# Sums of squares in column groups, wider rows of x, and four dots of the first shift on TensorE

## Chip, core and metric

The kernel runs on one core of a Trainium2 chip. The metric is the time of one execution on the device in microseconds (us); times are medians of three runs. Profiles show one execution: TensorE (PE) with its weight loads (PEld), VectorE (DVE), ScalarE (ACT), GpSimd (POOL), and the DMA queue of SyncE (SP).

## What is computed

Two layers over 1024 tokens of 1024 channels, in fp32, the first with a convolution as token mixer, the second with a pooling mixer:

```python
s = silu(c)
for i in range(2):
    sh, sc, gt = split(s @ w_mod[i] + b_mod[i], 3)
    h = rms(x, norm_g[i]) * (1 + sc) + sh
    if i == 0:                                   # _conv_mixer
        a, b, g = split(h @ w_in, 3)
        y = depthwise_conv31(a * sigmoid(b)) + db
        o = (silu(layernorm(y)) * silu(g)) @ w_out
    else:                                        # _pool_mixer
        v, g = split(h @ w_in, 2)
        p = window_means(v, (2, 4, 8, 16)) - v
        o = (grouped(p @ w_grp) * scale * silu(g)) @ w_out
    x = x + gt * o
```

`rms` and `layernorm` divide each token by the root of a mean of squares over its 1024 channels.

## The kernel before

Channels lie on the partitions, tokens along a row. x is a set of eight blocks of 128 channels, each in two halves `h` of 512 tokens. A product in fp32 is three matmuls (`mm3`, L200 to L203): each factor is split into a high and a low part of the type fp32r, a cast (`hi_part`, line L164 or L165, ScalarE) and a subtraction (`lo_part`, L169 or L170, VectorE or GpSimd). So `h10h` and `h10l` are the parts of the modulated x of half 1, blocks 0 and 1; `w00h` and `w00l` those of a weight.

Program order: load x of half 0 (eight DMAs of 256 KB), its norm, and block by block the modulation `mod_block` (two dots of `s_row`, the row of silu(c), with a block of `w_mod`, one for the shift and one for the scale, each one VectorE instruction, L287), `x <- x * a * rb` (L366), and `h`; seven accumulations `pf` on TensorE take up each block as it comes. Then half 1 is normed in the same way (`vax`, `vpx`, `rbx`), and the `pg` products use both halves. The 31 taps of the convolution run as products `pr` on ScalarE with adds `z` on GpSimd (L471, L472) and as `cv` chains on VectorE (L484); TensorE goes through the other products (`ps`, `psg`) meanwhile. `layernorm` follows for each half: means by `mr` and `mu`, squares `sqz`, their sums `vpz`, `rbz`. Then `gate_norm`, `out_half` (products `pso`, which give the x of the second layer, whose squares are `sqy`, sums `vpy`, factor `rby`), `h2_half`, and the second layer with `psv`, `psq`, `psy`, `psf`.

Five norms need, for each token, a sum over 1024 channels, that is over partitions as well. There are two forms. In `squares` (x0, x1, y1) VectorE adds up the squares of the eight blocks (L266) and four matmuls with a moving operand of a single column add over the partitions; y1 keeps its last block apart and has eight. In `square_sums` (z0, z1, y0) each block of squares has its own four such matmuls (L277), the block being the stationary operand. Both leave the sums as 128 x 4. `rstd_rows` turns these into the factor: ScalarE adds eps (`ve`, L240), GpSimd takes the power -0.5 (`vr`, L242), ScalarE spreads it on four diagonals (`dg`, L247), one matmul makes a row block of it (`rb`, L248). Names carry the norm: `vex`, `vry`, `dgz`.

Four tile pools matter: PSUM tag "ax" is one single bank (sums, `rb`, `gv`), "mm" has five and "cv" two; the SBUF ring for squares, "sq", has two buffers, as has that of the products, "pr".

The order on each engine is fixed when the program is built: a scheduler takes instructions by priority, by its own estimate of when they are ready (`priority(-LATER)` puts the norms first; `behind` and `ordered` add constraints). On the chip each engine takes its list in that order and waits at an instruction whose operands aren't there. An edit in one place therefore reorders others.

## Time and profile before

| what | value |
|---|---|
| median of three runs | 758.52 us (757.62 to 759.13) |
| the profiled execution's own time | 758.71 us |
| its span, first to last instruction | 756.9 us |
| TensorE busy | 724.2 us (96%) |
| VectorE busy | 532.1 us (70%) |
| ScalarE busy | 386.4 us (51%) |
| GpSimd busy | 435.4 us (58%) |
| chain that ended last, by engine | PE 70%, DVE 14%, POOL 8%, ACT 3% |

A busy share is a mean over stages that differ. Where a stretch of the trace shows one engine busy all the time, that engine sets the pace there; elsewhere one looks for what it waits for.

### The profile page before, as it was taken

How to read it: one execution, taken by the hardware profiler on the slowest of the kernel's cores; microseconds unless marked ns; L12 is line 12 of the kernel's file. 1: busy time of each engine (PE TensorE's matmuls, PEld its weight loads, DVE VectorE, ACT ScalarE, POOL GpSimd, SP SyncE). 2: the span in 40 equal slices, each digit the busy share in tenths (PEclk: the TensorE clock that was granted, in tenths of full speed). 3: DMA queues.
4: the chain of work that ended last, by engine and by line, in shares of the span. 5: the costliest groups of instructions: out<-in, count | busy, mean ns of one | idle time of the engine just before them, and what ended most of it. 6: DMA issues, size and time to landing. Idle time of an engine off the chain costs nothing.

```text
span 756.9 us, 9894 instructions
## 1 busy us (share of the span) xinstructions
PE 724.2 (96%) x3572; PEld 574.1 (76%) x3572; DVE 532.1 (70%) x724; ACT 386.4 (51%) x576; POOL 435.4 (58%) x377
## 2 busy tenths in 40 slices
PE   3899999999999999999989989999999999999998
PEld 1677786676768788778766768788888788888997
DVE  5997997889898941589969989671737364477321
ACT  5355556656613346876886676652414433334110
POOL 2000889999913438899998999763117413344232
PEclk9999999999999999999999989999999999999999
DMA  8882006466323441643650132445625610334132
GB/s 324 315 318 82 0 1 249 167 223 233 132 82 98 152 153 63 202 140 113 207 171 24 57 126 83 154 168 160 203 92 203 200 56 28 98 112 140 56 126 72
DMA packets 36481, 105.68 MB, mean 140 GB/s; under 512 B 4048, under 2 KB 6224, under 8 KB 36432
## 3 DMA queue, kind: packets, MB, share of 16 engines
q1 hardware_dynamic: 36432, 105.05, 40.8%
q8 instruction: 28, 0.46, 0.2%
q14 instruction: 21, 0.17, 0.1%
HBM read 92.45 MB, written 12.58 MB: 139 GB/s over the span
## 4 chain that ended last, share of the span: by engine, by line
PE 70%; DVE 14%; POOL 8%; ACT 3%; issue 2%; DMA 2%; SPq 0%; DVEq 0%; POOLq 0%; ACTq 0%
POOL z L472 8%; PE ps L201 4%; PE ps L203 4%; PE ps L202 4%; PE psf L202 4%; PE psf L203 4%; PE psf L201 4%; PE psv L203 3%; PE psv L202 3%; PE psv L201 3%; PE psq L202 3%; PE psq L201 3%; PE psq L203 3%; PE psg L203 3%; PE psg L201 3%; PE psg L202 3%
## 5 line engine op out<-in xcount | busy, mean ns | idle before, releaser
L472 POOL TENSOR_TENSOR z<-z,pr 128x512 f32<-128x512 f32 (+8 forms) x210 | 297.1, 1415 | 49.4 <-ACT pr L471 21.2
L471 ACT ACTIVATE pr<-y,VT 128x512 f32<-128x512 f32 (+8 forms) x210 | 150.2, 719 | 96.8 <-POOL z L472 90.2
L484 DVE SCALAR_TENSOR_TENSOR cv<-y,VT,cv 128x512 f32<-128x512 f32 (+12 forms) x261 | 175.4, 741 | 0.4
L770 DVE SCALAR_TENSOR_TENSOR xf<-psf,gt,xf 128x260 f32<-128x260 f32 (+1 forms) x24 | 13.2, 570 | 36.9 <-PE psf L203 31.4
L753 DVE SCALAR_TENSOR_TENSOR q<-psy,VT,q 128x260 f32<-128x260 f32 (+1 forms) x24 | 13.6, 571 | 31.9 <-PE psy L203 31.7
L242 POOL TENSOR_TENSOR vrx<-vex,mhalf 128x4 f32<-128x4 f32 x2 | 2.1, 1026 | 57.2 <-ACT vex L240 57.2
L567 DVE TENSOR_TENSOR z<-z,rbz 128x512 f32<-128x512 f32 x16 | 10.7, 680 | 28.9 <-PE rbz L248 28.9
L671 DVE TENSOR_TENSOR s<-v 128x535 f32<-128x535 f32 x8 | 12.3, 1536 | 19.5 <-ACT v L719 19.5
L675 DVE TENSOR_TENSOR s<-s 128x517 f32<-128x517 f32 (+5 forms) x24 | 20.9, 870 | 0.6
L559 ACT ACTIVATE gn<-z,VT 128x512 f32<-128x512 f32 x16 | 12.4, 777 | 14.6 <-DVE z L567 14.4
L287 DVE SCALAR_TENSOR_TENSOR wmb<-wmb,s_row 128x1024 f32<-128x1024 f32 x16 | 19.4, 1220 | 0.0
L583 DVE SCALAR_TENSOR_TENSOR xr<-pso,gt,xr 128x512 f32<-128x512 f32 x16 | 11.5, 741 | 10.7 <-PE pso L203 10.7
L299 PE MATMUL gv<-wk,srep 128*32 128x256 f32 x256 | 18.6, 388 | 0.0
L164 ACT CAST y<-q 128x504 fp32r<-128x504 f32 (+1 forms) x16 | 9.9, 618 | 16.8 <-DVE q L753 16.8
L169 DVE TENSOR_TENSOR y<-q,y 128x504 fp32r<-128x504 f32 (+1 forms) x16 | 13.9, 869 | 3.6 <-ACT y L164 3.6
L277 PEld LDWEIGHTS vpz<-ones,sqz 128*128 128x128 f32 x128 | 15.5, 191 | 0.7
L275 ACT ACTIVATE sqz<-z 128x512 f32<-128x512 f32 x16 | 9.8, 629 | 12.0 <-PE vpz L277 11.5
L202 PE MATMUL psy<-pd,grs 128*128 128x260 f32 (+1 forms) x48 | 15.3, 320 | 0.0
L203 PE MATMUL psy<-pd,grs 128*128 128x260 f32 (+1 forms) x48 | 15.3, 319 | 0.0
L201 PE MATMUL psy<-pd,grs 128*128 128x260 f32 (+1 forms) x48 | 15.1, 318 | 0.0
L277 PE MATMUL vpz<-ones,sqz 128*128 128x1 f32 x128 | 14.7, 245 | 0.0
L169 DVE TENSOR_TENSOR grs<-gr,grs 128x512 fp32r<-128x512 f32 x8 | 9.1, 1132 | 8.0 <-ACT grs L164 8.0
(2503 smaller groups left out, 2352.6 us busy)
## 6 DMA issues: line engine op xcount, KB each, us to landing
wk<-in_wk SPq DMA_DIRECT2D x32, 512.0 KB, 5.1
wmb<-in_wm SPq DMA_DIRECT2D x16, 512.0 KB, 6.4
wo<-in_cv_wo SPq DMA_DIRECT2D x16, 512.0 KB, 3.5
wp<-in_pl_wo SPq DMA_DIRECT2D x16, 512.0 KB, 3.5
wg<-in_cv_w SPq DMA_DIRECT2D x12, 512.0 KB, 3.7
wv<-in_pl_w SPq DMA_DIRECT2D x12, 512.0 KB, 3.4
wq<-in_pl_w SPq DMA_DIRECT2D x12, 512.0 KB, 3.5
x<-in_xT SPq DMA_DIRECT2D x16, 256.0 KB, 6.2
```

The lines of the kernel that those rows point to most:

```text
L169: return eng.tensor_tensor(out=lo, in0=src, in1=hi.bitcast(F32), op=ALU.subtract)
L201: nc.tensor.matmul(ps, w[0], r[0], start=first, stop=False)
L202: nc.tensor.matmul(ps, w[0], r[1], start=False, stop=False)
L203: nc.tensor.matmul(ps, w[1], r[0], start=False, stop=last)
L277: nc.tensor.matmul(vp[:, j : j + 1], sq[:, bl(j)], ones[:, 0:1], start=i + j == 0, stop=i == KT - 1, skip_group_check=True,)
L287: nc.vector.scalar_tensor_tensor(out=w, in0=w, scalar=1.0, in1=s_row, op0=ALU.mult, op1=ALU.mult, accum_out=out)
L299: nc.tensor.matmul(ps[32 * q : 32 * q + 32, :256], srep[:, kt, :], w[:, 256 * q : 256 * q + 256], start=kt == 0, stop=kt == KT - 1,)
L471: nc.scalar.activation(pr[:, o], y[:, i], AF.Copy, scale=dw(k))
L472: nc.gpsimd.tensor_tensor(out=z[:, o], in0=z[:, o], in1=pr[:, o], op=ALU.add)
L484: nc.vector.scalar_tensor_tensor(out=a[:, o], in0=y[:, i], scalar=dw(k), in1=a[:, o], op0=ALU.mult, op1=ALU.add)
L675: nc.vector.tensor_tensor(out=s[:, :m], in0=s[:, :m], in1=s[:, step : step + m], op=ALU.add)
L753: mixed[0] = nc.vector.scalar_tensor_tensor(out=sg[m][:, piece], in0=ps, scalar=vcol(ct, V_PS), in1=sg[m][:, piece], op0=ALU.mult, op1=ALU ...
```

## The change

1. All five norms take their sums by `token_sums`: for each block of squares four matmuls with a stationary operand of 32 columns of `onesd` (all 1/1024), each on another quarter of the 512 tokens, written to another 32 partitions of PSUM: four column groups. The result is 128 x 128, a token in each column of a group. `squares` with its adds on VectorE goes.
2. `rstd_rows` therefore gets two more steps: a copy `vrow` of the 128 x 128 with eps (ScalarE) and a matmul with `sel` that picks one row of each group and gives 128 x 4; `ve` becomes a copy.
3. x is laid out by the host so that two blocks lie side by side in one row: four DMAs of 512 KB with rows of 4 KB in place of eight of 256 KB with rows of 2 KB, in `load_x` and in `out_half`.
4. For the blocks 1 to 4 (`SH_PE`) the dot for the shift leaves VectorE. `dot_pe` has eight matmuls with `srep` (32 equal columns of silu(c)) in four column groups, over the block of `w_mod` in another layout, a copy `shrow` on ScalarE, and a matmul with `selm` that adds the groups; VectorE adds the bias from PSUM.

```diff
@@ -27,6 +27,7 @@
 CORD = [ct for p in PAIRS for ct in p]
 FILL = (4, 6, 5, 7)
 MIX_AT = 4
+SH_PE = (1, 2, 3, 4)
 EARLY_W = (1, 1, 2, 2)
 EARLY_AT = (0, 2, 1, 1)
 EARLY_ENG = ((0, 0, 0, 0), (1, 1, 1, 1))
...
-    RINGS = {"w": 4, "raw": 4, "sg": 2, "sq": 2, "pr": 2, "vs": 1}
+    RINGS = {"w": 4, "raw": 4, "sg": 2, "sq": 2, "pr": 2}
     WIDTH = {"E": 2 * NB, "Z": 2 * (NB + 2 * PAD), "sg": NB + 2 * PAD, "pr": NB}
     LATER = 1 << 20
     tc.cur_priority = 4 * LATER
@@ -101,13 +102,6 @@
 
     def bl(j):
         return slice(j * P, (j + 1) * P)
-
-    def packed(tags, name):
-        res = []
-        for j, tag in enumerate(tags):
-            u = unit(tag, f"{name}{j}")
-            res += [u[:, hs(0)], u[:, hs(1)]]
-        return res
 
     def pair(region, i, name):
         return unit(f"{region}{i}", name + "h", F32R), unit(f"{region}{i + 1}", name + "l", F32R)
@@ -222,24 +216,22 @@
 
     power_done, spread_done = [None], [None]
 
-    def rstd_rows(total, name):
-
-
-        sums, vp = total
-        if vp is None:
-            vp = axps(f"vp{name}")
-            with priority(-LATER):
-                for i, summed in enumerate(sums):
-                    for j in range(4):
-                        nc.tensor.matmul(
-                            vp[:, j : j + 1], summed[:, bl(j)], ones[:, 0:1], start=i + j == 0,
-                            stop=i == len(sums) - 1, skip_group_check=True,
-                        )
-        ve = S.tile([P, 4], F32, tag="ve", name=f"ve{name}", bufs=2)
+    def token_sums(ps, src, first, last):
+
+
+        for j in range(4):
+            nc.tensor.matmul(ps[32 * j : 32 * j + 32, :P], onesd[:, :32], src[:, bl(j)], start=first, stop=last)
+
+    def rstd_rows(vp, name):
+
+        row = S.tile([P, P], F32, tag="vrow", name=f"vrow{name}", bufs=1)
+        rs = S.tile([P, 4], F32, tag="vr", name=f"vr{name}", bufs=2)
         with priority(-LATER):
-            nc.scalar.activation(ve, vp[:, 0:4], AF.Identity, scale=1.0 / D, bias=eps)
-        rs = S.tile([P, 4], F32, tag="vr", name=f"vr{name}", bufs=2)
-        power_done[0] = nc.gpsimd.tensor_tensor(out=rs, in0=ve, in1=mhalf[:, 0:4], op=ALU.pow)
+            nc.scalar.activation(row, vp[:, :P], AF.Identity, bias=eps)
+            nc.tensor.matmul(vp[:, P : P + 4], row, sel, start=True, stop=True)
+            ve = S.tile([P, 4], F32, tag="ve", name=f"ve{name}", bufs=2)
+            nc.scalar.copy(ve, vp[:, P : P + 4])
+            power_done[0] = nc.gpsimd.tensor_tensor(out=rs, in0=ve, in1=mhalf[:, 0:4], op=ALU.pow)
         rb = axps(f"rb{name}")
         dg = half("sq", f"dg{name}")
         with priority(-LATER):
@@ -249,38 +241,16 @@
         spread_done[0] = spread
         return rb, done
 
-    def squares(xs, name, apart=False):
-
-        total = half("vs", f"va{name}")
-        sums = [total]
-
-        def add(i):
-            if i == 0:
-                nc.scalar.activation(total, xs[i], AF.Square)
-                return None
-            sq = half("sq", f"sq{name}{i}")
-            nc.scalar.activation(sq, xs[i], AF.Square)
-            if apart and i == KT - 1:
-                sums.append(sq)
-                return None
-            return nc.vector.tensor_tensor(out=total, in0=total, in1=sq, op=ALU.add)
-
-        return (sums, None), add
-
     def square_sums(xs, name, vp):
 
 
         def add(i):
             sq = half("sq", f"sq{name}{i}")
             done = nc.scalar.activation(sq, xs[i], AF.Square)
-            for j in range(4):
-                nc.tensor.matmul(
-                    vp[:, j : j + 1], sq[:, bl(j)], ones[:, 0:1], start=i + j == 0, stop=i == KT - 1,
-                    skip_group_check=True,
-                )
+            token_sums(vp, sq, i == 0, i == KT - 1)
             return done
 
-        return (None, vp), add
+        return vp, add
 
     def dot(w, out):
 
@@ -320,12 +290,14 @@
     xs = [None, None]
 
     def load_x(h):
-        xs[h] = packed([f"{'FZ'[h]}{j}" for j in range(4)], f"x{h}")
-        for kt in range(KT):
-            load_next(xs[h][kt], xT[bl(kt), hs(h)])
+        xs[h] = []
+        for j in range(4):
+            u = unit(f"{'FZ'[h]}{j}", f"x{h}{j}")
+            load_next(u, xT[h, j])
+            xs[h] += [u[:, hs(0)], u[:, hs(1)]]
 
     def norm_x(h):
-        total, add = squares(xs[h], f"x{h}")
+        total, add = square_sums(xs[h], f"x{h}", axps(f"vpx{h}"))
         for kt in range(KT):
             last = add(kt)
         return last, rstd_rows(total, f"x{h}")[0]
@@ -341,11 +313,26 @@
         nc.tensor.matmul(ps, ones, dg, start=True, stop=True)
         nc.scalar.copy(s_row[:, hs(h)], ps)
 
+    def dot_pe(kt, w):
+
+        ps = axps(f"sh{kt}")
+        row = S.tile([P, P], F32, tag="vrow", name=f"shrow{kt}", bufs=1)
+        with priority(-LATER):
+            for k in range(KT):
+                g = slice(32 * (k % 4), 32 * (k % 4) + 32)
+                nc.tensor.matmul(ps[g, :P], srep[:, k, :], w[:, bl(k)], start=k < 4, stop=k >= 4)
+            nc.scalar.copy(row, ps[:, :P])
+            nc.tensor.matmul(ps[:, P : P + 1], row, selm[:, 0:1], start=True, stop=True)
+        return ps[:, P : P + 1]
+
     def mod_block(kt):
         dots = []
         for part in range(2):
             w = unit("w" if part else "raw", f"wmb{kt}{part}")
             load_next(w, wm[part, kt])
+            if part == 0 and kt in SH_PE:
+                dots.append(dot_pe(kt, w))
+                continue
             dots.append(S.tile([P, 1], F32, tag=f"dot{part}", name=f"dot{kt}{part}", bufs=2))
             dot(w, dots[part])
         nc.vector.tensor_tensor(out=sh0[:, kt : kt + 1], in0=dots[0], in1=vcol(kt, V_BM), op=ALU.add)
@@ -574,10 +561,12 @@
 
     def out_half(h, y1, ws, done, beside=None):
         group = len(ws)
-        x1 = packed([f"Z{j}" for j in range(4)], f"xr{h}")
-        for m in range(KT):
-            nc.sync.dma_start(out=x1[m], in_=xT[bl(m), hs(h)])
-        total, add = squares(x1, f"y{h}", True) if h else square_sums(x1, f"y{h}", axps("vpy0"))
+        x1 = []
+        for j in range(4):
+            u = unit(f"Z{j}", f"xr{h}{j}")
+            nc.sync.dma_start(out=u, in_=xT[h, j])
+            x1 += [u[:, hs(0)], u[:, hs(1)]]
+        total, add = square_sums(x1, f"y{h}", axps(f"vpy{h}"))
 
         def finish(m, ps):
             nc.vector.scalar_tensor_tensor(
@@ -857,11 +846,14 @@
     )
     wk = np.stack([g["w_mod"][i][:, j * D : (j + 1) * D] for i, j in ((0, 2), (1, 0), (1, 1), (1, 2))])
     wk = wk.reshape(4, KT, P, D)
+    wm = g["w_mod"][0].T.reshape(3, KT, P, D)[:2].copy()
+    for kt in SH_PE:
+        wm[0, kt] = wm[0, kt].reshape(P, KT, P).transpose(2, 1, 0).reshape(P, D)
     wf = g["cv_w_in"][0].reshape(KT, P, 3, D)[:, :, :2, : FIRST * P]
     arrays = {
-        "xT": g["x"][0].T,
+        "xT": g["x"][0].T.reshape(4, 2, P, 2, HW).transpose(3, 0, 2, 1, 4).reshape(2, 4, P, 2 * HW),
         "vecs": vecs,
-        "wm": g["w_mod"][0].T.reshape(3, KT, P, D)[:2],
+        "wm": wm,
         "wk": wk,
         "cv_first": wf.reshape(KT, P, 2 * FIRST * P),
         "cv_w": tiles(g["cv_w_in"][0]),
```

The lists of the engines change with it. TensorE at the end of the first `pf` stage, before (`rbx` carries the factor of half 1 to all partitions, `pg` are products of half 0 first and of `h10` after them):

```order
L202 MATMUL pf_200<-h06l,w07h 128x512
L203 MATMUL pf_200<-h06h,w07l 128x512
L248 MATMUL rbx_531<-dgx_532,ones 128x512
L201 MATMUL pg_628<-h00h,w00h 128x512
L202 MATMUL pg_628<-h00l,w00h 128x512
L203 MATMUL pg_628<-h00h,w00l 128x512
L201 MATMUL pg_628<-h00h,w01h 128x512
```

and after:

```order
L195 MATMUL pg_708<-h06h,w07h 128x512
L196 MATMUL pg_708<-h06l,w07h 128x512
L197 MATMUL pg_708<-h06h,w07l 128x512
L240 MATMUL rbx_611<-dgx_612,ones 128x512
L195 MATMUL pg_737<-h10h,w00h 128x512
L195 MATMUL pg_762<-h10h,w00h 128x512
L195 MATMUL pg_790<-h10h,w00h 128x512
L195 MATMUL pg_815<-h10h,w00h 128x512
L195 MATMUL pg_843<-h10h,w00h 128x512
```

Before, 24 matmuls of one `pg` on the blocks of half 0 follow `rbx` before the first with `h10h`; now these 24 stand ahead of `rbx`. Its `sel` stands 19 matmuls ahead of it.

VectorE at the same place, before (`x <- x,a,rbx` is the modulation of half 1, `cv` the convolution, `h10l` the low part for TensorE):

```order
L382 TENSOR_TENSOR y_588<-pf_195,sig_589 128x512
L480 TENSOR_SCALAR cv_1043<-y_588,VT 128x512
L480 TENSOR_SCALAR cv_1044<-y_588,VT 128x511
L370 SCALAR_TENSOR_TENSOR x_447<-x_447,a_128,rbx_531 128x512 x2
L370 SCALAR_TENSOR_TENSOR x_448<-x_448,a_128,rbx_531 128x512 x2
L370 SCALAR_TENSOR_TENSOR x_449<-x_449,a_128,rbx_531 128x512 x2
L370 SCALAR_TENSOR_TENSOR x_450<-x_450,a_128,rbx_531 128x512 x2
L484 SCALAR_TENSOR_TENSOR cv_1043<-y_588,VT,cv_1043 128x497
L482 MEMSET cv_1044 128x1
L170 SCALAR_TENSOR_TENSOR h10l<-x_447,sh_129,h10h 128x512 x2
```

and after:

```order
L471 SCALAR_TENSOR_TENSOR cv_1124<-y_668,VT,cv_1124 128x504
L369 TENSOR_TENSOR y_733<-pg_708,sig_734 128x512
L471 SCALAR_TENSOR_TENSOR cv_1123<-y_668,VT,cv_1123 128x505
L357 SCALAR_TENSOR_TENSOR x_507<-x_507,a_128,rbx_611 128x512 x2
L357 SCALAR_TENSOR_TENSOR x_509<-x_509,a_128,rbx_611 128x512 x2
L357 SCALAR_TENSOR_TENSOR x_511<-x_511,a_128,rbx_611 128x512 x2
L357 SCALAR_TENSOR_TENSOR x_513<-x_513,a_128,rbx_611 128x512 x2
L471 SCALAR_TENSOR_TENSOR cv_1124<-y_668,VT,cv_1124 128x506
L471 SCALAR_TENSOR_TENSOR cv_1123<-y_668,VT,cv_1123 128x507
L164 SCALAR_TENSOR_TENSOR h10l<-x_507,sh_129,h10h 128x512 x2
```

The eight x's stand behind nine `cv` and behind a `y` that reads a finished `pg`, and two `cv` instead of one stand between them and `h10l`.

TensorE near the second norm of half 1, before (`psf` are products of the second layer, `rby` the factor of y1):

```order
L202 MATMUL psf_5077<-y_4007,wp70h 128x504
L203 MATMUL psf_5077<-y_4007,wp70l 128x504
L201 MATMUL psf_5077<-y_4018,wp70h 128x504
L202 MATMUL psf_5077<-y_4018,wp70h 128x504
L203 MATMUL psf_5077<-y_4018,wp70l 128x504
L248 MATMUL rby_4997<-dgy_4998,ones 128x512
L201 MATMUL psf_5077<-y_4196,wp70h 128x504
```

and after:

```order
L197 MATMUL psf_5179<-y_4089,wp70l 128x504
L195 MATMUL psf_5179<-y_4100,wp70h 128x504
L196 MATMUL psf_5179<-y_4100,wp70h 128x504
L197 MATMUL psf_5179<-y_4100,wp70l 128x504
L231 MATMUL vpy_4779<-sel,vrowy_5092 128x4
L240 MATMUL rby_5099<-dgy_5100,ones 128x512
L195 MATMUL psf_5179<-y_4278,wp70h 128x504
L196 MATMUL psf_5179<-y_4278,wp70h 128x504
```

Before, 14 matmuls lie between the last sums `vpy` and `rby`; now 11 lie between the last sums and `sel`, and none between `sel` and `rby`. In the other norms the squares' sums move too: those of x1 from one block behind 147 matmuls of `pf` to eight blocks behind 84 to 148; those of z0 by 5, 10 and 15 matmuls back. On ScalarE `dgy` of y0 comes behind the cast `wv20h`, which it stood ahead of, and on GpSimd `vry` of y0 stands behind five more of the convolution's z's.

## Rows read from the trace of the kernel before

**Rows 1.** The page: busy time of each engine, share, instructions.

```profile
PE 724.2 (96%) x3572; PEld 574.1 (76%) x3572; DVE 532.1 (70%) x724; ACT 386.4 (51%) x576; POOL 435.4 (58%) x377
```

**Rows 2.** Stretches: length, busy time (records) of PE, PEld, DVE, ACT, POOL, clock, DMA, GB/s.

```profile
22.80:62.00 39.20, 38.10 (x156) 30.04 (x157) 37.87 (x66) 17.42 (x24) 0.00 (x0) 1.00 0.84 310
85.00:225.00 140.00, 140.00 (x779) 101.54 (x780) 125.63 (x189) 77.34 (x114) 116.50 (x86) 1.00 0.41 147
390.00:470.00 80.00, 73.87 (x302) 56.07 (x302) 74.76 (x85) 56.60 (x88) 74.32 (x76) 0.96 0.24 79
448.00:452.00 4.00, 3.56 (x8) 2.82 (x9) 2.25 (x3) 2.73 (x5) 3.87 (x4) 0.50 0.42 134
610.00:757.00 147.00, 143.31 (x850) 126.76 (x848) 68.87 (x90) 40.47 (x56) 45.39 (x44) 1.00 0.27 87
```

**Rows 3.** Waits of TensorE: who, for whom, us in total, times, longest.

```profile
PE pf L201 <- ACT h00h L165: 2.2, 1, 2.2
PE psv L203 <- DVE wv40l L169: 3.7, 1, 3.7
```

**Rows 4.** Time line of TensorE: start, us, engine, line, operation, records [idle before].

```profile
122.28 0.39 PE L202 MATMUL ps<-h04l,wb4h 128*128 128x512 f32 x1
122.50 0.40 PE L203 MATMUL ps<-h04h,wb4l 128*128 128x512 f32 x1
122.83 0.64 PE L299 MATMUL gv<-wk,srep 128*32 128x256 f32 x8
123.40 0.51 PE L201 MATMUL ps<-h04h,wb4h 128*128 128x512 f32 x1
123.74 0.39 PE L202 MATMUL ps<-h04l,wb4h 128*128 128x512 f32 x1
...
141.74 0.50 PE L308 MATMUL gv<-sel,row 128*128 128x4 f32 x4
142.10 0.49 PE L203 MATMUL ps<-h16h,wb4l 128*128 128x512 f32 x1
...
148.05 1.93 PE L299 MATMUL gv<-wk,srep 128*32 128x256 f32 x32
149.91 0.50 PE L201 MATMUL ps<-h00h,wb5h 128*128 128x512 f32 x1
...
349.19 0.95 PE L277 MATMUL vpy<-ones,sqy 128*128 128x1 f32 x8
350.00 0.47 PE L201 MATMUL pso<-y100h,wo06h 128*128 128x512 f32 x1
```

**Rows 5.** Time line of VectorE and ScalarE, end of the squares of x0.

```profile
10.59 3.08 DVE L266 TENSOR_TENSOR vax<-vax,sqx 128x512 f32<-128x512 f32 x4 [0.20 <-ACT sqx L262]
11.45 1.30 ACT L262 ACTIVATE sqx<-x 128x512 f32<-128x512 f32 x2
```

**Rows 6.** Time line of three engines around `rbx` of x1.

```profile
66.66 1.02 PE L248 MATMUL rbx<-dgx,ones 128*128 128x512 f32 x2
68.63 5.35 DVE L370 SCALAR_TENSOR_TENSOR x<-x,a,rbx 128x512 f32<-128x512 f32 x8
69.40 1.38 ACT L165 ACTIVATE h10h<-x,sh 128x512 fp32r<-128x512 f32 x2 [1.15 <-DVE x L370]
74.54 0.75 DVE L170 SCALAR_TENSOR_TENSOR h10l<-x,sh,h10h 128x512 fp32r<-128x512 f32 x1
75.35 0.50 PE L202 MATMUL pg<-h10l,w00h 128*128 128x512 f32 x1 [1.16 <-DVE h10l L170]
```

**Rows 7.** Time line of GpSimd and VectorE ahead of the second layer.

```profile
384.08 8.21 POOL L472 TENSOR_TENSOR z<-z,pr 128x512 f32<-128x512 f32 x5 [0.36 <-ACT pr L471]
389.04 2.10 DVE L169 TENSOR_TENSOR wv20l<-wv,wv20h 128x1024 fp32r<-128x1024 f32 x1 [2.93 <-ACT wv20h L164]
```

**Rows 8.** Time line of ScalarE, the factor of y1.

```profile
599.68 0.26 ACT L240 ACTIVATE vey<-vpy,eps 128x4 f32<-128x4 f32 x1 [5.23 <-PE vpy L234]
601.07 1.28 ACT L247 ACTIVATE dgy<-ident,vry 128x128 f32<-128x128 f32 x4 [1.12 <-POOL vry L242]
```

## The prediction, made before the changed kernel ran

> **What bounds the kernel now.** I read the page's busy line first: TensorE works in 724.2 of 756.9 us, 96% of the span [rows 1]. The page names a list of lines, none of them dominant, so the question is where the other engines set TensorE's pace. The table of stretches tells it: from 85 to 225 us TensorE is busy 140.0 of 140 us, from 610 to 757 us 143.31 of 147, but from 390 to 470 us only 73.87 of 80, while VectorE is at 74.76 and GpSimd at 74.32 [rows 2]. So in most of the program a microsecond of TensorE is a microsecond of time, and around 390 to 450 us it is not: there TensorE waits, the longest time 3.7 us for VectorE's `wv40l` [rows 3]. Behind that wait the granted clock reads 0.50 from 448 to 452 us [rows 2], 1.2 of 2.4 GHz: an idle stretch of that length costs twice.
>
> **What a block of sums costs on TensorE.** Fixed first, since every part uses it. Plain 512-column matmuls start 0.22 to 0.23 us apart. One group of four narrow matmuls (128 x 32 weights, 256 columns, 8 records) takes 0.57 us from its start to the next start; the start before it comes 0.10 late and the second one behind it 0.11 late: 0.78 in all [rows 4]. Four groups in one run take 1.86 us start to start, so a further group costs (1.86 - 0.57)/3 = 0.43 and each visit a fixed 0.35. The new groups have half the columns, 128. I take 0.43/2 = 0.22 for one, 0.56 for a visit with one group and 0.78 with two. Bounds: 0.22 (no fixed part) and 0.78 (columns don't matter). An old block of four one-column matmuls takes 0.81 and about 0.1 of border: 0.9; a pair 1.8. Two `sel` matmuls of four columns take 0.36 [rows 4]; I take that for each `sel` and `selm`.
>
> The Trainium skill ("TensorEngine Tiling (Array Packing)", Theoretical Speedup) gives up to a factor of four for a stationary of at most 32 columns, and its Key Properties say that a change of tiling mode drains the engine. The rows show 0.9 against 0.56, a factor of 1.6; with the factor of four, 0.22 a block, the sum would be that of rival 1.
>
> **A. The start, to the end of the seven `pf` accumulations.** Before, the first norm's last square ends at 11.45 + 1.30 = 12.75 us and the last add at 10.59 + 3.08 = 13.67 [rows 5]. The add goes (-0.9), two short copies on ScalarE and a `sel` are added (some +0.9), and ScalarE's squares now stand behind both `s_row` copies. I take -0.5, from -2 (the 4 KB rows land earlier) to +1. From 22.8 to 62 us TensorE is busy 38.10 of 39.20 us and VectorE 37.87 [rows 2]: VectorE loses seven adds per norm and four dots, but TensorE has 1.1 us to gain, not more. It is given: three dot visits of two groups (the fourth runs while `h00h` is awaited, 2.2 us [rows 3]), 3 x 0.78, and four `selm`, 4 x 0.36: +3.7. The squares of x1: three pairs, two singles and one pair torn apart by a plain matmul, 3 x 0.78 + 2 x 0.56 + 0.35 = 3.8 instead of one block of 0.9: +2.9. The dots share the one bank "ax" with the sums, and the next group stands one matmul behind a `selm` whose result VectorE must first add: three waits of some 0.5, less most of the 1.1: +0.3. A: **+6** (0 to +9; 0 with blocks at 0.22 and an early start).
>
> **B. `rbx` of x1.** This is the largest term. Before, 24 matmuls of `pg` stand between `rbx` and the first one that reads `h10h`, and TensorE waits 1.16 us, once, for `h10l` [rows 6]. In the new order these 24 stand ahead of `rbx`, and `pg<-h10h` right behind. Count from the end of the 24: `rbx` 1.0 us. VectorE first takes a `y` that needs the last of the 24, and one cv, some 0.7 each (the x's take 5.35/8 = 0.67): the x's start at +1.5. From the first x to `h10h` on ScalarE are 69.40 - 68.63 = 0.77 us, and 0.7 for that cast (1.38 for two): TensorE goes on at +3.0, idle 2.0. Five matmuls: +4.2. `h10l` stands behind all eight x's (5.35) and now two cv instead of one (1.4), then 75.35 - 74.54 = 0.8: +9.0, idle 4.8. Together 6.8, less 1.16: +5.7. The second gap is longer than the 3.7 us after which the clock read 0.50 for 4 us; the same again costs 2 us. One `sel`: +0.36. From 85 us on TensorE has no idle time to give this back. B: **+8** (+4.5 without the clock and with an early VectorE, +9.5 if its nine cv run late).
>
> **C. z0 and y0, 225 to 450 us.** Off TensorE come eight blocks of z0 (four pairs, 7.2, against 4 x 0.78: -4.1) and of y0 (7.2 against one pair and six singles, 4.1: -3.1); two `sel` come on. But here GpSimd's z's (384.08, five in 8.21 us [rows 7]) run without a break and ScalarE's products for them wait for these; the z0 squares were moved 5, 10 and 15 matmuls later, 1.2, 2.3 and 3.5 us, which uses up what each saved ahead of it, so the stream starts as late as before. I give the saving no effect. Against it, `vry` on GpSimd now stands behind five more z's, and ScalarE's `dgy` behind `wv20h`. Before, VectorE had multiplied two x's by `rby` and waited 2.93 us for `wv20h` until 389.04 [rows 7]. Now `vry` comes after those five z's, at 384.08 + 3 x 1.64 = 389.0 less the pow's own 1.1 [rows 8], so about 388 to 389; `dgy` and `rby` follow (1.28 and 1.0 [rows 6, 8]), x at 391 to 392, and `wv20l` behind two of them. That is 2 to 4 us later in a stretch where VectorE is full, less 0.67 for one add of the conv that `wv40l` no longer stands behind. C: **+3** (-2 if the saving of z0 pulls the stream forward, +5).
>
> **D. z1, 500 to 530 us.** TensorE-bound: four pairs, -4.1, one `sel`: **-3.7** (-5.3 to -2.5).
>
> **E. y1, near 600 us.** Eight single visits instead of two blocks of 0.9: +2.7. One `sel`, 0.36. And a wait: before, 14 matmuls cover the way from the sums to `rby`; in the new order `rby` stands directly behind `sel`. That way is `vey`, `vry`, `dgy`: from 599.68 to 601.07 + 1.28 = 602.35, 2.7 us, and 0.1 of handing over [rows 8]. Twelve matmuls behind `rby` cover the first h2 as before. E: **+5.9** (+3 to +8, the latter with a clock that falls).
>
> **Sum.** +6 + 8 + 3 - 3.7 + 5.9 = +19.2 on the profiled execution's own 758.71 us, 1.8 over its span: 777.9. The median shown, 758.52, is 0.2 lower: **777.7 us**. TensorE's work alone comes out level: -4.1 - 3.1 - 4.1 off, +2.7 + 2.9 + 3.7 and some 1.4 of `sel` on, -0.6; the waits decide.
>
> **Rivals.** 1. *Entering a column group is free*, a block costs 0.22. Then A is +3.5 (dots 2.7, x1 +0.8), D -5.1, E +3.1, C about +2.5, B +8: +12 or so, 770 us; with an early start of 2 us 768. For it: the ratio of 256 to 512 columns hides no fixed part inside a long run; against it: the late starts on both sides of each `gv` visit [rows 4]. 2. *Faster*: free entry, and z0's earlier end releases GpSimd's stream, so that z0's and y0's 11 us come through (C -10), B stays at 6 because the clock holds: A +2.7, D -5.1, E +3.1: -3.3, 755 us; with half of B hidden 751. It decides at the first z of conv(1,1): if that starts 3 us or more earlier behind the last `pg` than before. Against it: ScalarE and GpSimd are the ones waited for there, and the squares moved back. 3. *The dots don't relieve VectorE in time*: a `selm` waits for `shrow`, queued on ScalarE behind weight casts of 1 us, which at each of the four places costs a wait like the present one for `h10l`, 1.16 [rows 6]: 4.6 more, 782 us. 4. *No change*: VectorE, freed of 14 adds and 4 dots, reaches the x's of x1 as the shorter order has it, A is 0, C -2, B +4.5, D -5.3, E +3: 758.9.
>
> **How the numbers follow.** The forecast 0.60, rival 1 0.14, rival 2 0.13, rival 3 0.07, rival 4 0.06. A measurement tells 0.2%, about 1.5 us, from no change. Faster 0.13, the same 0.06, slower 0.81. The range takes in rivals 1, 3 and 4 and leaves out rival 2: the lower end 757, the upper end the sum with A +9, B +9.5, C +5, D -2.5, E +7, which is 28, less a bit as not all fall together: 786.
>
> **What would show it.** B: in the profile after, a wait of `pg` for `h10h` of about 2 us and one for `h10l` of about 5, close together near 80 us, and a granted clock under 1 behind them; without these the forecast falls by 8. E: TensorE waiting for `dgy` ahead of `rby` nearly 3 us. Block price: the start-to-start time of a `vpz` pair, 0.78 forecast with borders. A: how much later than 66.66 the last `pf` matmul is through, where `rbx` starts now [rows 6]. C: the start of `wv20l` or of the x's by `rby`, against `vry`. If TensorE's waits from 305 to 390 us don't grow by some 4 us, z0's saving came through and C is wrong.

## The result and the profile after

The changed kernel takes **778.99 us** (median of four, 778.55 to 784.03) against 758.07 (757.44 to 759.13) before: the ratio is 1.029, with a 95% interval from 1.0245 to 1.0334. It is 20.9 us slower; the forecast was 777.7, which is 19.6 above this median of before. The profiled execution is the longest of the four, 784.03 us with a span of 782.2; 25.3 us over the profiled one of before. A second trace of the same kernel (below) took 782.67. All comparisons of two traces here are of such profiled executions, and the 4 to 5 us between them and the median come up again under A. In the runs below three executions lie far outside the others (814, 1088 and 2347 us); the medians and ratios here leave them out.

The page of the kernel after: busy time by engine, as in [rows 1].

```profile
PE 733.8 (94%) x3816; PEld 564.1 (72%) x3816; DVE 508.7 (65%) x696; ACT 389.1 (50%) x586; POOL 432.7 (55%) x377
```

TensorE is busy 9.6 us longer, VectorE 23.4 shorter, and the span is 25.3 longer: the other 16 us are idle time of TensorE. The 9.6 us are not all work; some of it is matmuls at a lower clock, such as those behind `rby` (E below). The stretches, with the columns of [rows 2]:

```profile
22.80:62.00 39.20, 34.09 (x209) 25.73 (x202) 27.56 (x50) 15.46 (x24) 0.00 (x0) 0.90 0.77 282
85.00:100.00 15.00, 8.74 (x25) 6.61 (x26) 14.62 (x22) 8.11 (x12) 4.30 (x3) 0.66 0.00 0
92.00:98.00 6.00, 5.32 (x13) 4.16 (x14) 6.00 (x9) 1.74 (x3) 2.38 (x2) 0.50 0.00 0
130.00:270.00 140.00, 140.00 (x784) 99.70 (x784) 118.84 (x181) 72.23 (x102) 101.13 (x72) 1.00 0.48 166
417.00:470.00 53.00, 49.73 (x212) 37.51 (x211) 53.00 (x63) 35.48 (x55) 45.00 (x48) 1.00 0.18 60
626.00:634.00 8.00, 8.00 (x24) 5.95 (x23) 5.49 (x8) 3.67 (x5) 3.50 (x2) 0.67 0.17 59
```

From 130 to 270 us TensorE is busy all the time, as it was from 85 to 225: a loss ahead of it is not given back there. From 85 to 100 it works 8.74 of 15 us, and from 92 to 98 at a granted clock of 0.50, the lower of its two levels (1.2 of 2.4 GHz); from 626 to 634 the mean is 0.67. Before, TensorE waited 1.16 us at the first of these places in the program and not at all at the second. From 417 to 470 VectorE is busy all 53 us.

Those of TensorE's waits that the text below uses, as in [rows 3]:

```profile
PE rby L240 <- ACT dgy L239: 7.2, 2, 4.6
PE sh L323 <- DVE sh L338: 5.0, 1, 5.0
PE pg L196 <- DVE h10l L164: 4.4, 1, 4.4
PE pg L195 <- ACT h10h L159: 2.2, 1, 2.2
PE pso L195 <- ACT y102h L158: 2.0, 2, 1.0
```

Before, `rby` had 0.7, `h10l` 1.2 and `y102h` 0.3 us; the waits for `sh` and `h10h` are new.

One finds the loss by setting the start of the same matmul in both traces side by side. How much later it starts in the kernel after:

| place (first matmul of the kind) | before | after | later by |
|---|---|---|---|
| first `pf` | 22.80 | 23.24 | 0.4 |
| first `pg`, at the end of `pf` | 67.12 | 77.83 | 10.7 |
| `pg <- h16h,w07l`, behind both waits | 85.33 | 104.14 | 18.8 |
| `psg <- h00h,wg20h` | 269.76 | 288.32 | 18.6 |
| `psg <- h06h,wg30l`, behind z0's sums | 299.60 | 311.92 | 12.3 |
| `pso <- y102h,wo00h` | 317.63 | 337.47 | 19.8 |
| `psq <- h206h,wq60l`, second layer | 497.32 | 518.82 | 21.5 |
| `psf <- wp50h`, behind z1's sums | 542.02 | 559.70 | 17.7 |
| `psf <- wp70h`, ahead of `rby` | 600.04 | 618.87 | 18.8 |
| `psv <- h210h`, behind `rby` | 606.37 | 631.67 | 25.3 |

The two lines that part A from B, before and then after:

```profile
67.12 0.80 PE L201 MATMUL pg<-h00h,w00h 128*128 128x512 f32 x1
85.33 0.40 PE L203 MATMUL pg<-h16h,w07l 128*128 128x512 f32 x1
```

```profile
77.83 0.39 PE L195 MATMUL pg<-h00h,w00h 128*128 128x512 f32 x1
104.14 0.40 PE L197 MATMUL pg<-h16h,w07l 128*128 128x512 f32 x1
```

### The profile page after: what moved, and what is told of

It is laid out like the page before. It is cut to its first block, busy times and chain, and to the rows that moved or that the text cites. A ratio compares the mean times of both kernels' runs of the same rounds, so it can differ in the third digit from the quotient of the medians.

```text
span 782.2 us, 10348 instructions
## 1 busy us (share of the span) xinstructions
PE 733.8 (94%) x3816; PEld 564.1 (72%) x3816; DVE 508.7 (65%) x696; ACT 389.1 (50%) x586; POOL 432.7 (55%) x377
## 4 chain that ended last, share of the span: by engine, by line
PE 69%; POOL 10%; DVE 9%; ACT 5%; issue 3%; DMA 3%; SPq 0%; POOLq 0%; ACTq 0%; DVEq 0%
POOL z L459 9%; PE ps L197 4%; PE ps L195 4%; PE ps L196 4%; PE psf L196 4%; PE psf L195 4%; PE psf L197 4%; PE psg L195 3%; PE psg L196 3%; PE psg L197 3%; PE psq L197 2%; PE psq L195 2%; PE psq L196 2%; DVE cv L471 2%; PE psv L197 2%
## 5 line engine op out<-in xcount | busy, mean ns | idle before, releaser
L471 DVE SCALAR_TENSOR_TENSOR cv<-y,VT,cv 128x512 f32<-128x512 f32 (+11 forms) x261 | 175.7, 743 | 0.4
L554 DVE TENSOR_TENSOR z<-z,rbz 128x512 f32<-128x512 f32 x16 | 10.7, 679 | 26.2 <-PE rbz L240 26.1
L664 DVE TENSOR_TENSOR s<-s 128x517 f32<-128x517 f32 (+5 forms) x24 | 25.5, 1062 | 0.6
L572 DVE SCALAR_TENSOR_TENSOR xr<-pso,gt,xr 128x512 f32<-128x512 f32 x16 | 11.6, 744 | 20.9 <-PE pso L197 20.9
L660 DVE TENSOR_TENSOR s<-v 128x535 f32<-128x535 f32 x8 | 12.3, 1538 | 19.5 <-ACT v L708 19.5
L257 DVE SCALAR_TENSOR_TENSOR wmb<-wmb,s_row 128x1024 f32<-128x1024 f32 x12 | 14.6, 1222 | 13.0 <-DMA wmb<-in_wm 6.5
L603 DVE SCALAR_TENSOR_TENSOR xr<-xr,a,rby 128x512 f32<-128x512 f32 x16 | 11.6, 738 | 14.0 <-PE rby L240 14.0
L546 ACT ACTIVATE gn<-z,VT 128x512 f32<-128x512 f32 x16 | 12.3, 774 | 13.3 <-DVE z L554 13.3
L269 PE MATMUL gv<-wk,srep 128*32 128x256 f32 x256 | 18.6, 388 | 0.0
L476 DVE TENSOR_TENSOR z<-z,cv 128x512 f32<-128x512 f32 x9 | 6.1, 682 | 11.9 <-ACT z L475 11.9
L673 POOL TENSOR_TENSOR s<-s,ecol 128x1 f32<-128x1 f32 (+5 forms) x14 | 3.6, 257 | 17.7 <-DVE s L664 14.4
```

Of the source, the lines that this page charges most:

```text
L257: nc.vector.scalar_tensor_tensor(out=w, in0=w, scalar=1.0, in1=s_row, op0=ALU.mult, op1=ALU.mult, accum_out=out)
L269: nc.tensor.matmul(ps[32 * q : 32 * q + 32, :256], srep[:, kt, :], w[:, 256 * q : 256 * q + 256], start=kt == 0, stop=kt == KT - 1,)
L471: nc.vector.scalar_tensor_tensor(out=a[:, o], in0=y[:, i], scalar=dw(k), in1=a[:, o], op0=ALU.mult, op1=ALU.add)
L664: nc.vector.tensor_tensor(out=s[:, :m], in0=s[:, :m], in1=s[:, step : step + m], op=ALU.add)
```

## The order around rbx of x1 (B)

The same place as in [rows 6], kernel after, three engines:

```profile
83.63 1.02 PE L240 MATMUL rbx<-dgx,ones 128*128 128x512 f32 x2
84.07 0.68 DVE L369 TENSOR_TENSOR y<-pg,sig 128x512 f32<-128x512 f32 x1
85.32 5.35 DVE L357 SCALAR_TENSOR_TENSOR x<-x,a,rbx 128x512 f32<-128x512 f32 x8
86.09 1.38 ACT L159 ACTIVATE h10h<-x,sh 128x512 fp32r<-128x512 f32 x2 [4.21 <-DVE x L357]
86.86 1.43 PE L195 MATMUL pg<-h10h,w00h 128*128 128x512 f32 x5 [2.22 <-ACT h10h L159]
90.58 1.39 DVE L471 SCALAR_TENSOR_TENSOR cv<-y,VT,cv 128x506 f32<-128x506 f32 x2
91.89 1.40 DVE L164 SCALAR_TENSOR_TENSOR h10l<-x,sh,h10h 128x512 fp32r<-128x512 f32 x2
92.69 0.79 PE L196 MATMUL pg<-h10l,w00h 128*128 128x512 f32 x1 [4.39 <-DVE h10l L164]
93.28 0.63 PE L197 MATMUL pg<-h10h,w00l 128*128 128x512 f32 x1
93.70 0.63 PE L195 MATMUL pg<-h10h,w01h 128*128 128x512 f32 x1
```

`rbx` is through at 84.6. VectorE has its `y` and a cv in front, so the eight x's start at 85.32; `h10h` follows 0.77 later, and TensorE, which has nothing but `pg <- h10h` next, waits 2.22 us. The five matmuls that don't need `h10l` last to 88.3; `h10l` comes behind eight x's and two cv, at 92.69 on TensorE, a wait of 4.39. Behind it the matmuls start 0.42 to 0.43 apart in place of 0.23. The forecast had 2.0 and 4.8 us, and 2 us for the clock.

To see what the wait costs, one kernel takes away the reason for it: x of half 1 is multiplied by a row that is there long before, so that its own norm is left out of the result.

```diff
-            nc.vector.scalar_tensor_tensor(out=x, in0=x, scalar=a, in1=rbs[1], op0=ALU.mult, op1=ALU.mult)
+            nc.vector.scalar_tensor_tensor(out=x, in0=x, scalar=a, in1=s_row[:, hs(1)], op0=ALU.mult, op1=ALU.mult)
```

> The changed kernel, but the x of half 1 is multiplied by the row of silu(c) in place of its own factor rbx (so the norm of half 1 is left out of the result, though all of it is computed): h10h and h10l no longer wait for rbx. Step B says that the order around rbx costs 8 us with the clock that falls behind it: 779.0 less 8, 771, with no wait for h10h or h10l near 90 us and a granted clock of 1 there. If those waits only show time that is lost anyway further down, 777 to 779.

Measured: 771.7 us (769.25 to 773.36 over three executions; ratio 1.0176, 1.0151 to 1.0202): 7.3 less than the changed kernel. In its trace `h10l` costs no wait, and this stretch runs at full clock:

```profile
75.00:85.00 10.00, 10.00 (x43) 7.79 (x42) 8.62 (x15) 7.37 (x13) 8.30 (x7) 1.00 0.00 1
85.00:100.00 15.00, 15.00 (x66) 12.18 (x66) 10.81 (x18) 6.76 (x11) 10.89 (x9) 1.00 0.00 1
```

From 85 to 100 us TensorE is busy all 15 us (8.74 before the edit), at a clock of 1.00. So the edit is worth 7.3 of the 20.9 us by this run, and the order around `rbx` 8.1 by the trace (18.8 - 10.7). The two are not quite the same thing. The edit also moves other sums of x1 and reorders the `pg` products: from the first `pg` to `psg <- h00h,wg20h` its trace takes 199.5 us, the changed kernel's 210.5, but the one before only 202.6, so it takes away 3.2 us that the order never cost. By the same difference of two places the second trace of the changed kernel gives 7.3, and the kernel with two dots (under A), which has the same two waits (2.05 and 4.39 us), 6.5. Between 6.5 and 8.1 is what the record supports.

## The sums, one norm at a time

Four kernels are the one before with the new form for some norms alone (`GROUPS`); narrow rows of x, dots on VectorE. The main lines of the edit:

```diff
+GROUPS = ("z1",)      # the others: ("z0", "y0"); ("y1",); ("x0", "x1")
...
             done = nc.scalar.activation(sq, xs[i], AF.Square)
+            if name in GROUPS:
+                token_sums(vp, sq, i == 0, i == KT - 1)
+                return done
             for j in range(4):
...
```

**z1.**

> The kernel before with column groups for the sums of z1 alone. By the step D of the prediction this saves four pairs at 1.8 less 0.78 and costs one sel, -3.7 us: 754.4 against 758.1. If entering a column group were free it would be -5.1 (753). If the factor rbz, which now stands 33 matmuls later, is late for pso, little or nothing is left (757 to 758). A vpz pair should take 0.78 us from start to start with its borders, against 1.8 before.

Measured: 757.4 us against 757.7; ratio 0.9992 (0.9983 to 1.0002). No gain. The price of a block was right; TensorE in this kernel, a pair of z1's squares among 504-column matmuls:

```profile
505.60 0.38 PE L204 MATMUL psf<-y,wp10h 128*128 128x504 f32 x1
505.91 0.65 PE L230 MATMUL vpz<-sqz,onesd 128*32 128x128 f32 x16
506.49 0.49 PE L205 MATMUL psf<-y,wp10h 128*128 128x504 f32 x1
506.82 0.39 PE L206 MATMUL psf<-y,wp10l 128*128 128x504 f32 x1
```

The pair takes 0.58 from start to start, and the starts on both sides come 0.31 and 0.33 after the one ahead, not 0.23: 0.76, where 0.78 was forecast and 1.8 is the old price. A single visit in the y1 kernel takes 0.36 and the same borders: 0.55 against 0.56. So the saving is there: `psf <- wp50h` starts 2.7 us and `pso <- y110h,wo12h` 3.65 us earlier than before. Then it goes: `pso <- y110h,wo17l` starts only 0.9 earlier. The waits of that trace name the place:

```profile
PE pso L206 <- POOL wo17l L172: 2.3, 1, 2.3
```

Before, TensorE waited 0.5 us for `wo17l`, which GpSimd casts. Being earlier, it now waits 2.3. To see whether that takes the gain, the low parts of wo14 to wo17 go to VectorE, with z1 and, as a control, without:

```diff
-                w = load_split(cv_wo[m], f"wo{h}{m}", eng=(nc.vector, nc.gpsimd)[h])
+                w = load_split(cv_wo[m], f"wo{h}{m}", eng=nc.vector)
```

> The kernel before with column groups for z1 alone, and the low parts of the last four weights of the first layer's second half (wo14 to wo17) on VectorE and not on GpSimd. With z1 alone TensorE was 3.7 us ahead at 549 us and had lost 1.8 of it at 587, behind a wait of 2.3 us for wo17l on GpSimd. If that wait takes the gain back, it comes through here: 758 less 3 to 4, 754.5, against 757.5 for z1 alone. If something else further down takes it, 757.

> The kernel before with only those low parts moved to VectorE: the control for the run with z1. TensorE waits 0.5 us for wo17l before, so 757.5 to 758 (no change); anything faster than 757 would mean that the gain of the other run is not z1's.

Measured: with z1 756.0 us (754.55 to 762.6 over twelve runs; ratio 0.9993, 0.9972 to 1.0013), without 757.7 (ratio 1.0004, 0.9995 to 1.0012). The trace of the first has no wait for `wo17l` left and a span of 753.3 us, 3.6 below that of before, as expected, and 2.7 below the control's (756.0). But its executions fall into two groups, eight from 754.5 to 757.3 and four from 760.5 to 762.6, and the interval holds 1. The move alone does nothing. What lengthens some of the executions was not found; they have no trace. So the wait is shown to take 1.8 us of the gain in the trace; that it takes all of it is not shown.

**z0 and y0.**

> The kernel before with column groups for z0 and y0 alone. Step C: TensorE is spared 7 us of sums, but GpSimd's adds set the pace there and dgy of y0 comes late: +3 (761), with a wait of TensorE for dgy ahead of rby and VectorE multiplying by rby at about 391 in place of 384.7. Rival 2 (the saving comes through): 751 or less. If the saving is only hidden and dgy costs nothing: 758.

Measured: 759.8 us, ratio 1.0026 (1.0014 to 1.0037): 2.1 slower. The saving shows and goes again, in both kernels alike: in this one `psg <- h06h,wg30l` starts 7.9 us earlier than before and `pso <- y102h,wo00h` 0.3. In the kernel after the table shows the same, 18.6, 12.3 and then 19.8 later. Not all of these 6.3 us are a saving: in the new order `rbz` and ten products of `psg` that stood ahead of the place stand behind it, some 3.3 us that come again; the other 3.0 are three pairs at the price found. They go because TensorE then waits for `y100h`, `y101h` and `y102h`, 2.83 us in five waits where it had none; the chain that ended last runs there through GpSimd's `z` and the `pr` products on ScalarE that wait for it, and GpSimd is busy 23.18 of 25.55 us. At the turn into the second layer, GpSimd before, then GpSimd, ScalarE, TensorE and VectorE in the kernel after, to be set beside [rows 7]:

```profile
379.82 1.02 POOL L242 TENSOR_TENSOR vry<-vey,mhalf 128x4 f32<-128x4 f32 x1
```

```profile
404.71 1.02 POOL L234 TENSOR_TENSOR vry<-vey,mhalf 128x4 f32<-128x4 f32 x1
405.41 1.03 ACT L158 CAST wv20h<-wv 128x1024 fp32r<-128x1024 f32 x1
406.83 1.26 ACT L239 ACTIVATE dgy<-ident,vry 128x128 f32<-128x128 f32 x4
408.15 2.07 PE L240 MATMUL rby<-dgy,ones 128*128 128x512 f32 x2 [4.56 <-ACT dgy L239]
410.26 1.41 DVE L603 SCALAR_TENSOR_TENSOR xr<-xr,a,rby 128x512 f32<-128x512 f32 x2 [6.63 <-PE rby L240]
411.59 1.22 DVE L163 TENSOR_TENSOR wv20l<-wv,wv20h 128x1024 fp32r<-128x1024 f32 x1
```

`vry` runs at 404.71, 24.9 us later than the old one, `dgy` behind the cast of `wv20h`, TensorE waits 4.56 us for it, and `wv20l` starts at 411.59, 22.5 later than 389.04, where TensorE's products ahead of it are 16 to 19.5 later: some 4 us lost, of which one is given back by 497 us. The table says +2.9 for the whole stretch (18.6 to 21.5), the forecast +3. In the kernel with z0 and y0 alone TensorE waits 3.02 us at this place and VectorE's x by `rby` starts at 390.24 (expected: about 391).

A last kernel keeps y0's old sums and has the groups for z0 and z1, wide rows, and the casts on VectorE; it asks whether z0's saving comes through when `dgy` stands where it stood.

> The kernel before with column groups for z0 and z1, those low parts on VectorE, and the wide rows of x. z0's 3.7 us should be hidden behind GpSimd's adds (rival 2 would give them), wide rows do nothing that the other runs show: 754.5 as with z1 alone; 751 if z0's saving comes through once y0 keeps its old sums and dgy stands where it stood.

Measured: 759.6 us, ratio 1.0021 (1.0010 to 1.0033), slower than before, and than the kernel with z1 and the casts (756.0, ratio 0.9993) by 3.6 us by the medians and 2.1 by the ratios. Its trace has no wait for `dgy` of y0. Rival 2 falls: z0's saving does not come through with y0 out of the way either, and something in this kernel costs time: z0's new order, or the wide rows, which no run has alone.

**y1.**

> The kernel before with column groups for y1 alone. Step E: eight single visits in place of two blocks, +2.7, a sel, +0.4, and a wait for dgy right ahead of rby, +2.8: +5.9 (764). Without the wait 761; with free entry into column groups 761 too, but then the wait is in the trace and the visits are cheap.

Measured: 764.4 us, ratio 1.0089 (1.0072 to 1.0106): +6.7. The way to `rby` in the kernel after, TensorE and ScalarE, to be set beside [rows 8]:

```profile
622.16 0.28 PE L231 MATMUL vpy<-sel,vrowy 128*128 128x4 f32 x2
622.48 0.16 ACT L233 COPY vey<-vpy 128x4 f32<-128x4 f32 x1 [2.44 <-PE vpy L231]
623.77 1.28 ACT L239 ACTIVATE dgy<-ident,vry 128x128 f32<-128x128 f32 x4 [1.12 <-POOL vry L234]
625.10 2.08 PE L240 MATMUL rby<-dgy,ones 128*128 128x512 f32 x2 [2.65 <-ACT dgy L239]
626.18 1.41 PE L195 MATMUL psf<-y,wp70h 128*128 128x504 f32 x1
627.39 0.62 PE L196 MATMUL psf<-y,wp70h 128*128 128x504 f32 x1
```

`sel` at 622.16, `vey`, `dgy`, `rby` at 625.10: TensorE waits 2.65 us; the forecast had 2.8. Behind it `rby` takes 2.08 us, not 1.02, and the next matmuls 0.62, not 0.39: the clock fell (0.67 from 626 to 634), which the forecast had only as the upper end. Before, the row was:

```profile
602.78 1.02 PE L248 MATMUL rby<-dgy,ones 128*128 128x512 f32 x2
```

What the clock is worth can be read from three traces with the same wait of 2.65 us. From the first `psf <- wp70h` to `psv <- h210h` TensorE needs 9.9 us in the kernel with no dot (under A), 11.5 with y1 alone and 12.8 in the kernel after; before it was 6.3. In the 8 us that begin 1 us after the start of `rby` the clock reads 1.00, 0.79 and 0.68. So its fall costs 0, 1.6 and 2.9 us.

**x0 and x1.**

> The kernel before with column groups for the two norms of x alone (narrow rows, dots on VectorE). Here rbx of x1 stands with 12 of the 24 pg matmuls behind it and not with none. Steps A and B without the dots: x1's squares +2.9, start -0.5, and half of the wait: the wait for h10h is covered, the one for h10l is about 4 us and the clock falls behind it: +6 to +7 (764.5). If the place of rbx did not matter, +2 to +3 (761).

Measured: 766.0 us (ratio 1.0112, 1.0094 to 1.0129): +8.3, some 1.5 more than forecast. The first `pf` starts 1.1 us later than before, not 0.5 earlier, and the matmuls behind `rbx` end 6.8 later; the wait for `h10l` is 3.7 and there is none for `h10h`, since 12 matmuls still stand behind `rbx`: half of the 24 cover the first wait and not the second.

## The dots (A)

By the table 10.7 us are lost up to the first `pg`; the forecast had 6. Four kernels bear on it: the changed one again for a second trace; the dots alone on the kernel before; the changed one with no dot on TensorE; and with two.

```diff
-SH_PE = (1, 2, 3, 4)
+SH_PE = ()          # two dots: (3, 4); the dots alone: (1, 2, 3, 4) with GROUPS = ()
```

> The changed kernel once more, for a second trace: its profiled execution took 784.0 us where three others took 778.6 to 779.3. If the 5 us are an accident of the first 45 us (TensorE waited 5.0 us for the shift of block 2, VectorE meanwhile for a transfer of w_mod), this one shows a shorter wait there and 778 to 780; if they belong to the kernel, again about 784.

> The kernel before with the four dots on TensorE alone. Step A's price: three visits at 0.78 and four selm at 0.36, +3.7 (761.8). If the dots' weights are held longer, because TensorE reads them only behind rbx and the ring of four buffers stops the loads of w_mod behind them, the wait for the shift of block 2 shows here too, with the DMA queue standing still between about 20 and 23 us: +4 to +8 (762 to 766). rbx of x1 stands far ahead in this order, so term B should not appear.

> The changed kernel with all dots on VectorE again: sums of all five norms in groups, wide rows. The single parts so far came to -0.3 (z1), +2.1 (z0 and y0), +6.7 (y1) and +8.9 (x0 and x1), together +17.4 (775.5). If wide rows do nothing and the parts add up, 775; if the wide rows bring the start of x forward, 774; if the dots are what pushes rbx behind all of pg and cost more than the difference to 779.0, below 772.

> The changed kernel with two dots on TensorE (blocks 3 and 4) in place of four. rbx of x1 stands where it stood, directly ahead of pg on h10h. If only the price of the dots counts, two visits and two selm less, one of the visits hidden: -1.5, 777.5. If the loads of w_mod are held back by the buffer that block 1's dot keeps until TensorE is past rbx, that hold goes too (the loads of block 3 should be issued near 18 us and not at 23, and TensorE's wait of 2.7 to 5.0 us for a shift should shrink to under 1): 773 to 775.

Measured: again 782.67 us with a wait of 5.0 once more; the dots alone 766.95 (ratio 1.0123, 1.0106 to 1.0140), +9.0; no dot 770.8 (1.0168, 1.0153 to 1.0183); two dots 774.0 (1.0215, 1.0201 to 1.0230). So four dots cost 8.2 us, of which those of blocks 1 and 2 are 5.0. By the price of the visits these two should have cost 1.5. The four parts of the sums, each alone on the kernel before, add up by their ratios to 2.2% (-0.08 + 0.26 + 0.89 + 1.12), and the kernel with no dot, which has all four and the wide rows, is 1.7% slower: the combination costs 4 us less. Of these 1.6 can be the clock, which doesn't fall behind its `rby`; the runs don't tell the rest. Not all of the 8.2 us belong to A either: without dots 12 of the 24 matmuls stand behind `rbx`, and TensorE has no wait for `h10h` and one of 3.46 us for `h10l`. With two dots and with four none stand there.

What the price leaves out is in the DMA queue. The issues of `w_mod` and the first weights on SyncE, kernel after, then with two dots (start, time to issue them, what):

```profile
12.96 0.80 SPq L184 DMA_DIRECT2D wmb<-in_wm  x2
16.46 0.33 SPq L184 DMA_DIRECT2D w<-in_cv_first  x1
23.37 0.80 SPq L184 DMA_DIRECT2D wmb<-in_wm  x2
```

```profile
12.99 0.80 SPq L184 DMA_DIRECT2D wmb<-in_wm  x2
16.49 0.33 SPq L184 DMA_DIRECT2D w<-in_cv_first  x1
17.63 0.80 SPq L184 DMA_DIRECT2D wmb<-in_wm  x2
```

The pair of loads for block 3 goes out at 23.37 us with four dots and at 17.63 with two (at 18.10 with none; before at 19.32; with the dots alone at 22.25). It takes the buffer of block 1's `w_mod` in the ring "raw" of four. VectorE's dot was done with it as soon as it had come; TensorE's reads it at 22.23, because its PSUM bank is the single "ax", which `rbx` and the x that reads it hold until then. The loads behind stand too: SyncE issues none from 16.8 to 23.4. The DMA engines are busy 7% of the time from 20.0 to 23.3 us (98% with two dots), and VectorE, freed of work as it was meant to be, waits for the transfers, and TensorE for VectorE's addition (the kernel after, VectorE and TensorE):

```profile
22.23 1.08 PE L323 MATMUL sh<-wmb,srep 128*32 128x128 f32 x16 [1.46 <-DVE x L353]
29.58 1.23 DVE L257 SCALAR_TENSOR_TENSOR wmb<-wmb,s_row 128x1024 f32<-128x1024 f32 x1 [2.42 <-DMA wmb<-in_wm]
39.89 1.23 DVE L257 SCALAR_TENSOR_TENSOR wmb<-wmb,s_row 128x1024 f32<-128x1024 f32 x1 [2.17 <-DMA wmb<-in_wm]
41.25 1.08 PE L323 MATMUL sh<-wmb,srep 128*32 128x128 f32 x16 [5.02 <-DVE sh L338]
```

The row at 39.89 stands on VectorE ahead of the addition of block 2's shift, which frees the bank for block 3's group: TensorE waits 5.02 us, and its group then takes 1.08 us in place of 0.65, a clock that fell. With two dots TensorE has no such wait, and the first `pg` starts 2.8 us later than before, not 10.7. With the dots alone it waits 2.56 us for the same addition.

This may be where the kernel's executions differ. Both traces with a wait of 5.0 took 782.7 and 784.0; the trace of the kernel without `rbx`, which is the same up to there, has 2.7 and no drop of the clock, and the first `pg` 9.8 later than before. That is 0.9 to 1.4 less than in those two. From `psf <- wp70h` to `psv <- h210h` it needs 11.5 us where both need 12.8. The runs with two dots lie within 0.3 us of each other (773.76 to 774.07). The three executions of 778.6 to 779.3 may have had the shorter wait; it is not shown, and these two differences come to less than the 4 to 5 us.

## Why the prediction was right, and where it was not

The time was forecast at 777.7 and is 779.0. In the traces the loss is 25.3 us where the steps add up to 19.2. By steps:

- **What bounds the kernel:** right. TensorE-bound stretches passed every loss on (18.8 us later at 104, 18.6 at 288), and the stretch with GpSimd and VectorE in it swallowed TensorE's saving. One reading was carried too far: [rows 7] shows GpSimd without a break at 384 us, but around z0, from `psg <- h00h,wg20h` to `pso <- y102h` (269.8 to 317.6 us), the trace of before has TensorE busy 47.87 of 47.87 us and GpSimd 31.49.
- **Price of a block:** right. 0.76 for a pair and 0.55 for a single one were measured, 0.78 and 0.56 forecast (1.8 and 0.9 in the old form, a factor of 2.4 and 1.6); rival 1 (free entry, 0.22) falls with it. A single `sel` was priced at 0.36 and takes about 0.2.
- **A:** mis-sized, +6 against +10.7 in the trace (+11.2 in the second). The price of the visits was there; what failed is that a dot that moves to another engine also keeps its operand's buffer until that engine reads it. I had named the bank "ax" as a wait of 0.5 between groups, and not asked who loads into the buffer of `w_mod` next. The start was +0.4, forecast -0.5. Rival 3 had the dots relieve VectorE too late, but by a late `shrow`; TensorE has no wait for `shrow` in the trace.
- **B:** right, in place, size and cause: +8 forecast, 6.5 to 8.1 in three traces, 7.3 by taking the wait away (with other things). The two gaps were 2.2 and 4.4 us, 2.0 and 4.8 in the forecast, with the clock at 0.50 behind the second.
- **C:** right in the number, +2.9 for +3; alone on the kernel before the two norms cost 2.1. The wait for `dgy` is there, but the kernel that keeps y0's old sums, without that wait, still loses 1.9 us from `pso <- y102h` to `psq <- h206h,wq60l`. And in the other traces with all the new sums the stretch from `psg <- h00h,wg20h` to `psq` costs between 2.0 and 6.0 us (6.0 with no dot). That the forecast met 2.9 is in part luck; what spreads it is open.
- **D:** right in the changed kernel, -3.8 (21.5 to 17.7) for -3.7. Its trace has no wait for `wo17l`, and that with y1 alone has none either. Alone, z1 gave 0.3 and not 3.7; the wait for `wo17l` on GpSimd took 1.8 of it in the trace. The forecast called the stretch bound by TensorE and did not ask what was late next; with y1's sums in the kernel as well it did not matter.
- **E:** +7.6 in the trace (17.7 to 25.3), +6.7 alone, +5.9 forecast. Of it 1.1 come ahead of `psf <- wp70h`: those are y1's visits, since with y1 alone the same place starts 1.2 later. The term that was left out of the sum is the clock, 2.9 us; without it E would be 4.7, below the forecast.

So the traced sum is 6.1 us too small, A by 4.7 and E by 1.7, the others within 0.2. The median comes out 1.3 us from the forecast only because the three executions without a profile are 4.7 to 5.5 us shorter than the traced one; no run shows which step is shorter in them, and to this extent the closeness is luck. Rival 4 (no change) falls with the time. None of the experiments gave a kernel that is clearly faster than the one before; the nearest, z1 with the casts on VectorE, is not told apart from it.

## What to carry to other kernels

A saving on the busiest engine is worth what the next engine allows (z1 alone: 3.65 us ahead at one place, 0.3 in the time): find, for each stage that it lies in, who is waited for once it is there, and move that too or leave the stage alone. When an operation moves to another engine, follow its operand's buffer: the load that takes that buffer next waits for the new reader, and the loads that the queue has behind it wait as well. And read the new order for work that used to stand between a long chain and its reader; the 24 matmuls that moved to the other side of `rbx` cost 6.5 to 8.1 us, more than the new sums saved at any one place.

## What was not expected of the hardware

Whether the clock falls behind a wait does not follow from the length of the wait alone. Ahead of `rby` TensorE waits 2.65 us in several kernels, for the same chain. In the changed kernel `rby` then ran slowly (2.08 us), and so did what follows. With y1 alone it ran at full clock (1.12 us), and the matmuls behind it started 0.41 to 0.43 us apart for 3 us. With no dot nothing slowed down. Behind 2.69 us for a shift in the kernel without `rbx` the group ran in 0.64, as at full clock. TensorE with no dot, then without `rbx`:

```profile
614.88 1.12 PE L266 MATMUL rby<-dgy,ones 128*128 128x512 f32 x2 [2.65 <-ACT dgy L265]
```

```profile
39.16 0.64 PE L323 MATMUL sh<-wmb,srep 128*32 128x128 f32 x16 [2.69 <-DVE sh L338]
```
